# A two-layer streaming-encoder trunk on one Trainium2 core: a fixed schedule for the sums, roundings and low parts of the left operands in the up projection's background

## The chip, the cores and the metric

One NeuronCore of a Trainium2 chip runs the whole program in one launch. The metric is device time in microseconds (us), the median of the runs shown. The engines are named as in the profile: PE (TensorE, matmul), PEld (its weight load), DVE (VectorE), ACT (ScalarE), POOL (GpSimd) and SP (SyncE, which issues the DMAs).

## The reference, cut to what matters

The trunk has two layers over a sequence of 1024 rows of width 1024. Each layer adds an S5 group and a differential attention group, and then a convolutional gated feed-forward block. The change lies in the last one:

```python
def _conv_gated_ffn(h, w_up, w_conv, b_conv, w_down):
    seqlen = h.shape[1]
    up = h @ w_up
    padded = jnp.pad(up, ((0, 0), (CONV_WIDTH - 1, 0), (0, 0)))
    conv = b_conv + sum(w_conv[j] * padded[:, j:j + seqlen] for j in range(CONV_WIDTH))
    gate = conv[..., :FFN_DIM]
    val = conv[..., FFN_DIM:]
    return (jax.nn.silu(gate) * val) @ w_down
...
    for i in range(DEPTH):
...
        h = _rmsnorm(x, norm_ffn[i])
        x = x + _conv_gated_ffn(h, w_up[i], w_conv[i], b_conv[i], w_down[i])
    return _rmsnorm(x, norm_final)
```

## The kernel before, in words

Every fp32 operand of a large matmul is split into a rounded high part (ACT, a copy to fp32r) and a low part (DVE or POOL, the operand less its high part). Three matmuls then make one product of two splits: high by high, high by low, low by high (`mm3`, L440 to L442).

**The up projection** (`up`, L1366) works on 22 tiles f of 128 channels of the gate and the same 128 of the value. Each tile is a two by two block product done with seven block products instead of eight, in the order of `UP_ORDER`: 11, 12, s2, s1, s3, 22, s4. A block product is 4 times `mm3`, 12 matmuls of 128x512. The results are collected in `u0` and `u1` in SBUF: ACT copies the accumulator `upa` out after 11, s2 and s3; DVE adds or subtracts `upb` after 12, `upc` after s3 and s4, and `upd` after 22. The accumulator `upa` goes on after each copy, so product s2 may start only when ACT has copied product 11 out. Likewise `upc`, made by product s1 and read by DVE after s3, goes on in product s4, so s4 may start only when DVE has read it.

**The background.** After each of the seven products of a tile the program calls `bg.tick()`, which takes every queued generator one step further. `gate(f)` (L1402) is queued at the end of tile f and runs in the ticks of tile f+1: the convolution of the value half after product 11 (one ACT instruction with the centre tap, two DVE scalar_tensor_tensor), that of the gate half after product 12, Silu on ACT after s1, and the product of both on DVE after s3. When f is odd, a pair (f-1, f) of gated tiles is complete. It then becomes a left operand of the down projection, which also uses seven products, and `Seven.spill` (L331) prepares that operand: four sums of blocks (s1 = 21 + 22, s2 = s1 - 11, s3 = 11 - 21, s4 = 12 - s2), for each of the seven operands (11, 12, s2, s3, s1, 22, s4) a rounding on ACT and a low part on DVE, and a store to DRAM through SP. The spill of one pair starts in the tick of product 22 of the tile after the odd one and takes nine ticks. Below, the tile in which a spill starts is called the first tile, and the next one, in which it ends, the second. Nine pairs per layer are spilled; the last four tiles go another way.

**The right operands** are prepared at the same time for weights needed some seven products later, in the same split: ACT rounds, POOL makes the four sums and the seven low parts of each tile (`Ring`, `Seven.value` and `split`, L226).

**What sets the order.** The program text gives each tick's steps; a scheduler then puts the instructions of each engine into one list, which the engine executes in order. That list is fixed when the program is built, so what stands in it is known before any run.

Of the kernel before, what the change touches and what calls it, by code (L numbers as in the profile page):

```python
# [10 lines left out]
F32R = mybir.dt.float32r  # L11
BF16 = mybir.dt.bfloat16
I32 = mybir.dt.int32
AF = mybir.ActivationFunctionType
# [30 lines left out]
TAIL = list(range(2 * NPAIR, NF))  # L45
UP_ORDER = ["11", "12", "s2", "s1", "s3", "22", "s4"]
DN_ORDER = ["11", "12", "s2", "s3", "s1", "22", "s4"]
PARTNER = {"11": "11", "12": "21", "s4": "22", "22": "t4", "s1": "t1", "s2": "t2", "s3": "t3"}


@with_exitstack
def trunk_kernel(ctx: ExitStack, tc: tile.TileContext, A: dict, out: bass.AP, dbg: dict):
# [12 lines left out]
    def s4(name):  # L65
        return P4.tile([128, 1024], F32, tag="s4", name=name)
# [29 lines left out]
    def act(o, i, f, **kw):  # L96
        return nc.scalar.activation(o, i, f, **kw)  # L97

    def tt(o, a, b, op):
        V.tensor_tensor(o, a, b, op=op)  # L100
# [7 lines left out]
    MUL, ADD, SUB = ALU.mult, ALU.add, ALU.subtract  # L108
# [7 lines left out]
    class Tasks:  # L116
# [3 lines left out]
        def store(self, dst, src):  # L120

            self.late.append((dst, src))
# [32 lines left out]
    store = bg.store  # L155
# [125 lines left out]
    class Seven:  # L281
# [48 lines left out]

        def spill(self, dst):  # L331

            todo, summed, rounded = list(DN_ORDER), None, None
            while todo or summed or rounded:
                if rounded:
                    (n, v, d), rounded = rounded, None
                    self.eng(n).tensor_tensor(d[:, 512:1024].bitcast(F32R), v, d[:, 0:512], op=SUB)  # L337
                    store(dst[n], d)
                if summed:
                    (n, v), summed = summed, None  # L340
                    d = s4("ao")
                    act(d[:, 0:512].bitcast(F32R), v, AF.Copy)
                    rounded = n, v, d
                if todo:
                    n = todo.pop(0)
                    summed = n, self.value(n)
                yield

    class Held:
# [46 lines left out]
    for l in range(DEPTH):  # L396
# [26 lines left out]
        for np_ in PAIRS:  # L423
            sv = []
            for p in range(p0, p0 + np_):
# [3 lines left out]
                sv.append(Seven(W, "t", src, h[1], lambda name: G))  # L429
            for n in DN_ORDER:  # L430
                for q in range(np_):
                    sv[q].job(sv[q].srcs["11" if n == "11" else "22"][0], PARTNER[n])
            p0 += np_
# [5 lines left out]
    def mm3(o, l, r, first, last, go_on=False):  # L439
        PE.matmul(o, l[0], r[0], start=first, stop=False, skip_group_check=go_on)  # L440
        PE.matmul(o, l[0], r[1], start=False, stop=False, skip_group_check=go_on)  # L441
        PE.matmul(o, l[1], r[0], start=False, stop=last, skip_group_check=go_on)  # L442
# [29 lines left out]
    def gbc(src, name):  # L472
        g = s4(name)
        dma(g, src.partition_broadcast(128))
        return g
# [36 lines left out]
    def rope_tables():  # L512
# [7 lines left out]
        for h in range(2):  # L520
# [12 lines left out]
    xd = [DR.tile([128, 1024], F32, name=f"xd{i}") for i in range(8)]  # L533
    ad = [[{n: DR.tile([128, 1024], F32, name=f"ad{l}_{p}_{n}") for n in DN_ORDER} for p in range(NPAIR)]
          for l in range(2)]
# [642 lines left out]
    for l in range(DEPTH):  # L1178
# [84 lines left out]
        gf = gbc(A["norm_ffn"][l], "gf")  # L1263
        B = {n: Pieces("b" + n, 2, 512) for n in PARTNER.values()}

# [85 lines left out]
        def product(o, n, first):  # L1351
            w = W.take()[0]
            for k in range(4):
                mm3(o, tuple(v[:, 128 * k:128 * k + 128] for v in w), B[PARTNER[n]].get(k, 0, 512),
                    first and k == 0, k == 3, not first)
# [75 lines left out]
        for np_ in PAIRS:  # L1431
            for n in DN_ORDER:
                for p in range(p0, p0 + np_):
# [28 lines left out]
        for np_ in PAIRS:  # L1462
            chain = None
            for n in DN_ORDER:
                As, Bs = A7.take(np_), W.take(np_)
# [5 lines left out]
                for t in range(4):  # L1471
                    if n in ("12", "22"):
                        o = (smt if t % 2 else bgt)("dn")
                    else:
                        o = chain[t // 2][:, 512 * (t % 2):512 * (t % 2) + 512]
# [6 lines left out]
                    lo, hi = slice(0, 512), slice(512, 1024)  # L1482
# [71 lines left out]
```

## Time and profile before

| | us |
|---|---|
| median of 3 runs | 2517.65 (2516.12 to 2517.66) |
| the profiled execution's own time | 2518.42 |
| its span, first to last instruction | 2516.7 |
| PE busy in the span | 2332.9 (93%) |
| DVE busy | 1762.1 (70%) |
| POOL busy | 1160.1 (46%) |
| ACT busy | 1112.7 (44%) |

The busy shares are averages over stages with different limits. A row of a timeline gives start, duration, engine, line, operation, output <- inputs, and in brackets the idle time of the engine just before and what ended it. Names have their buffer numbers left out: `w` on DVE is the pair of sums s1 and s2 of a spill, `ao` a split operand of a spill, `g` a gated tile, `c` a convolution's result, `op` a split weight.

### The profile page before, as it was taken

The page shows a single profiled execution, that of the slowest core. Times are in us where ns is not written, and L with a number is a line of the kernel's source. Part 1 is how long each engine was busy: PE and PEld are TensorE (multiplying, and loading weights), DVE is VectorE, ACT ScalarE, POOL GpSimd, SP SyncE. Part 2 cuts the span into 40 slices and gives each one's busy share as a digit, 9 for nine tenths or more (in the row PEclk, how much of TensorE's full clock was granted, in tenths as well). Part 3 has the DMA queues.
Part 4 walks back from the last instruction along what each step waited for, and adds up shares of the span by engine and source line. Part 5 has one row for each costly group of instructions (what it writes and reads, how often), then busy time and mean ns, then how long its engine had stood idle before and what let it go on. Part 6 is the DMA issues. An engine that isn't in the chain of part 4 may idle for free. (4 is left out here: it accounts for less than half of the span.)

```text
span 2516.7 us, 34975 instructions
## 1 busy us (share of the span) xinstructions
PE 2332.9 (93%) x12180; PEld 1933.9 (77%) x12180; DVE 1762.1 (70%) x3249; ACT 1112.7 (44%) x2164; POOL 1160.1 (46%) x853
## 2 busy tenths in 40 slices
PE   5899999997999999999988999999979999999998
PEld 4777987785887777777777788877858777777776
DVE  7987567658777878456579775675687787864645
ACT  4455266434555555322135642754245555552221
POOL 3210011035777878777022101012267788878750
PEclk8999999998999999999999999999989999999999
DMA  6344731421344435886134447214113444549651
GB/s 178 118 114 120 204 105 47 159 80 42 109 150 130 161 129 176 305 302 228 54 97 153 112 136 218 68 51 155 67 42 129 147 151 135 166 168 360 226 183 67
DMA packets 295753, 361.42 MB, mean 144 GB/s; under 512 B 43160, under 2 KB 230136, under 8 KB 295576
## 3 DMA queue, kind: packets, MB, share of 16 engines
q1 hardware_dynamic: 295576, 359.18, 43.5%
q8 instruction: 97, 1.59, 0.3%
q14 instruction: 80, 0.66, 0.1%
HBM read 235.36 MB, written 123.73 MB: 143 GB/s over the span
## 5 line engine op out<-in xcount | busy, mean ns | idle before, releaser
L231 POOL TENSOR_TENSOR op<-st,op 128x512 fp32r<-128x512 f32 x112 | 168.9, 1538 | 889.1 <-ACT op L97 815.2
L231 POOL TENSOR_TENSOR op<-wu,op 128x512 fp32r<-128x512 f32 x220 | 321.1, 1480 | 160.9 <-ACT op L97 159.0
L106 DVE SCALAR_TENSOR_TENSOR c<-u,cv,c 128x1023 f32<-128x1023 f32 (+1 forms) x176 | 230.2, 1310 | 57.0 <-ACT c L97 52.9
L440 PE MATMUL rw<-op,hTh 128*128 128x256 f32 x768 | 228.0, 297 | 8.3 <-ACT hTh L97 3.6
L441 PE MATMUL rw<-op,hTh 128*128 128x256 f32 x768 | 225.1, 293 | 1.6 <-POOL op L231 1.6
L442 PE MATMUL rw<-op,hTl 128*128 128x256 f32 x768 | 223.3, 291 | 0.0
L100 DVE TENSOR_TENSOR xf<-xf,dnc 128x512 f32<-128x512 f32 (+1 forms) x160 | 124.7, 792 | 132.0 <-PE dnc L442 121.9
L231 POOL TENSOR_TENSOR op<-w,op 128x512 fp32r<-128x512 f32 x124 | 175.0, 1422 | 24.9 <-ACT op L97 24.9
L97 ACT ACTIVATE c<-u,cv 128x1024 f32<-128x1024 f32 x88 | 106.7, 1212 | 149.6 <-DVE u L100 143.9
L231 POOL TENSOR_TENSOR op<-wd,op 128x512 fp32r<-128x512 f32 x106 | 138.1, 1322 | 68.2 <-ACT op L97 67.7
L440 PEld LDWEIGHTS rw<-op,hTh 128*128 128x128 f32 x768 | 151.4, 197 | 10.9 <-ACT hTh L97 4.0
L440 PE MATMUL dnc<-op,aop 128*128 128x512 f32 x360 | 146.6, 413 | 12.4 <-DVE xf L100 12.1
L441 PEld LDWEIGHTS rw<-op,hTh 128*128 128x128 f32 x768 | 151.4, 197 | 4.4 <-POOL op L231 2.5
L442 PEld LDWEIGHTS rw<-op,hTl 128*128 128x128 f32 x768 | 151.1, 197 | 0.7 <-issue 0.6
L441 PE MATMUL dnc<-op,aop 128*128 128x512 f32 x360 | 141.7, 394 | 0.0
L100 DVE TENSOR_TENSOR u<-u,upc 128x512 f32<-128x512 f32 x88 | 60.0, 681 | 115.3 <-ACT u L97 109.2
L442 PE MATMUL dnc<-op,aop 128*128 128x512 f32 x360 | 139.7, 392 | 0.0
L97 ACT ACTIVATE u<-upa 128x512 f32<-128x512 f32 x132 | 78.0, 591 | 139.1 <-PE upa L442 137.1
L97 ACT ACTIVATE op<-wu 128x512 fp32r<-128x512 f32 x220 | 129.0, 620 | 0.0
L337 DVE TENSOR_TENSOR ao<-g,ao 128x512 fp32r<-128x512 f32 x90 | 117.4, 1320 | 15.7 <-ACT ao L97 15.7
L97 ACT ACTIVATE op<-wd 128x512 fp32r<-128x512 f32 x106 | 62.3, 625 | 148.9 <-PE dnc L442 64.0
L97 ACT ACTIVATE e<-sc,anm 128x256 f32<-128x256 f32 (+7 forms) x128 | 94.1, 738 | 62.9 <-DVE anm L103 48.8
(341 smaller groups left out, 7133.1 us busy)
## 6 DMA issues: line engine op xcount, KB each, us to landing
wu<-in_w_up_dram SPq DMA_DIRECT2D x88, 512.0 KB
ad_s<-ao SPq DMA_DIRECT2D x72, 512.0 KB
aop<-ad_s SPq DMA_DIRECT2D x72, 512.0 KB
ad<-ao SPq DMA_DIRECT2D x54, 512.0 KB
aop<-ad SPq DMA_DIRECT2D x54, 512.0 KB
wd<-in_w_down_dram SPq DMA_DIRECT2D x44, 512.0 KB
st<-in_w_in_dram SPq DMA_DIRECT2D x32, 256.0 KB
st<-in_w_in_dram SPq DMA_DIRECT2D x16, 512.0 KB
```

The costliest lines, as they stand in the source:

```text
L97: return nc.scalar.activation(o, i, f, **kw)
L100: V.tensor_tensor(o, a, b, op=op)
L106: return V.scalar_tensor_tensor(o, a, s, b, op0, op1)
L231: eng.tensor_tensor(lo.bitcast(F32R), src, hi, op=SUB)
L337: self.eng(n).tensor_tensor(d[:, 512:1024].bitcast(F32R), v, d[:, 0:512], op=SUB)
L440: PE.matmul(o, l[0], r[0], start=first, stop=False, skip_group_check=go_on)
L441: PE.matmul(o, l[0], r[1], start=False, stop=False, skip_group_check=go_on)
L442: PE.matmul(o, l[1], r[0], start=False, stop=last, skip_group_check=go_on)
```

## The change

The spill no longer takes its operands one by one in a pipeline of three stages. A table, `SPILL`, says for each of the nine ticks which sums, roundings and low parts are done in it. The third and fourth ticks, in which the next tile's convolutions are started, have none. The same instructions are issued, all on the same engines: 4 sums and 7 low parts on DVE, 7 roundings on ACT, 7 stores.

```diff
+SPILL = [[("sum", "s1"), ("hi", "11")], [("sum", "s2"), ("lo", "11"), ("hi", "12")], [], [],
+         [("lo", "12"), ("sum", "s3"), ("hi", "s2")], [("lo", "s2"), ("sum", "s4"), ("hi", "s3")],
+         [("lo", "s3"), ("hi", "s1")], [("lo", "s1"), ("hi", "22"), ("hi", "s4")], [("lo", "22"), ("lo", "s4")]]
...
         def spill(self, dst):
 
-            todo, summed, rounded = list(DN_ORDER), None, None
-            while todo or summed or rounded:
-                if rounded:
-                    (n, v, d), rounded = rounded, None
-                    self.eng(n).tensor_tensor(d[:, 512:1024].bitcast(F32R), v, d[:, 0:512], op=SUB)
-                    store(dst[n], d)
-                if summed:
-                    (n, v), summed = summed, None
-                    d = s4("ao")
-                    act(d[:, 0:512].bitcast(F32R), v, AF.Copy)
-                    rounded = n, v, d
-                if todo:
-                    n = todo.pop(0)
-                    summed = n, self.value(n)
+            b, d = self.block, {}
+            self.tmp = s4("w7")
+            x, y = self.tmp[:, 0:512], self.tmp[:, 512:1024]
+            v = {"11": b("11"), "12": b("12"), "s1": x, "s2": y, "s3": b("21"), "22": b("22"), "s4": b("12")}
+            sums = {"s1": (x, b("21"), b("22"), ADD), "s2": (y, x, b("11"), SUB),
+                    "s3": (b("21"), b("11"), b("21"), SUB), "s4": (b("12"), b("12"), y, SUB)}
+            for step in SPILL:
+                for what, n in step:
+                    if what == "sum":
+                        o, p, q, op = sums[n]
+                        tt(o, p, q, op)
+                    elif what == "hi":
+                        d[n] = s4("ao")
+                        act(d[n][:, 0:512].bitcast(F32R), v[n], AF.Copy)
+                    else:
+                        tt(d[n][:, 512:1024].bitcast(F32R), v[n], d[n][:, 0:512], SUB)
+                        store(dst[n], d.pop(n))
                 yield
```

**DVE, from the first tile's products 22 and s4 into the second tile's product 12**, in the kernel before. The `u` rows with `upc`, `upd` and `upc` belong to products s3, 22 and s4 of the first tile, the one with `upb` to product 12 of the second; `c_8426` and `c_8456` are the two convolutions of the first tile.

```order
L100 TENSOR_TENSOR u_8262<-u_8262,upc 128x512
L337 TENSOR_TENSOR ao<-g,ao 128x512
L100 TENSOR_TENSOR u_8262<-u_8262,upd 128x512
L106 SCALAR_TENSOR_TENSOR c_8426<-u_8262,cv,c_8426 128x1023
L100 TENSOR_TENSOR u_8261<-u_8261,upc 128x512
L106 SCALAR_TENSOR_TENSOR c_8426<-u_8262,cv,c_8426 128x1022
L106 SCALAR_TENSOR_TENSOR c_8456<-u_8261,cv,c_8456 128x1023
L308 TENSOR_TENSOR w_8423<-g 128x512
L337 TENSOR_TENSOR ao<-g,ao 128x512
L309 TENSOR_TENSOR w_8423<-w_8423,g 128x512
L100 TENSOR_TENSOR u_8402<-u_8402,upb 128x512
```

The same place in the changed kernel (`u_8261` is now what `u_8262` was, and so on):

```order
L103 TENSOR_TENSOR w_8382<-g 128x512
L103 TENSOR_TENSOR u_8261<-u_8261,upc 128x512
L103 TENSOR_TENSOR w_8382<-w_8382,g 128x512
L103 TENSOR_TENSOR ao<-g,ao 128x512
L103 TENSOR_TENSOR u_8261<-u_8261,upd 128x512
L103 TENSOR_TENSOR ao<-g,ao 128x512
L103 TENSOR_TENSOR g<-g 128x512
L103 TENSOR_TENSOR g<-g,w_8382 128x512
L109 SCALAR_TENSOR_TENSOR c_8427<-u_8261,cv,c_8427 128x1023
L103 TENSOR_TENSOR u_8260<-u_8260,upc 128x512
L109 SCALAR_TENSOR_TENSOR c_8427<-u_8261,cv,c_8427 128x1022
```

All four sums and the low parts of 11 and 12 now stand ahead of the convolution's first scalar_tensor_tensor, the sums s3 and s4 and the low part of 12 though the table gives them to the fifth and sixth ticks; in the kernel before one low part stood there.

**DVE, in the second tile**, between the adding of `upb` (product 12) and of `upc` (product s3), in the kernel before:

```order
L100 TENSOR_TENSOR u_8402<-u_8402,upb 128x512
L319 TENSOR_TENSOR g<-g 128x512
L106 SCALAR_TENSOR_TENSOR c_8456<-u_8261,cv,c_8456 128x1022
L337 TENSOR_TENSOR ao<-w_8423,ao 128x512
L337 TENSOR_TENSOR ao<-g,ao 128x512
L337 TENSOR_TENSOR ao<-w_8423,ao 128x512
L325 TENSOR_TENSOR g<-g,w_8423 128x512
L100 TENSOR_TENSOR g<-g,c_8426 128x1024
L100 TENSOR_TENSOR u_8403<-u_8403,upc 128x512
```

and in the changed kernel:

```order
L103 TENSOR_TENSOR u_8408<-u_8408,upb 128x512
L103 TENSOR_TENSOR ao<-w_8382,ao 128x512
L103 TENSOR_TENSOR ao<-g,ao 128x512
L103 TENSOR_TENSOR g<-g,c_8427 128x1024
L103 TENSOR_TENSOR u_8409<-u_8409,upc 128x512
L103 TENSOR_TENSOR ao<-w_8382,ao 128x512
L103 TENSOR_TENSOR ao<-g,ao 128x512
L103 TENSOR_TENSOR u_8409<-u_8409,upd 128x512
L103 TENSOR_TENSOR ao<-g,ao 128x512
```

Two sums, one low part and a convolution step have left the stretch ahead of the adding of `upc`.

**ACT, the convolutions of the first tile and the copy of product 11 of the second**, in the kernel before:

```order
L97 ACTIVATE op_8404<-wu 128x512
L97 ACTIVATE c_8426<-u_8262,cv 128x1024
L97 ACTIVATE c_8456<-u_8261,cv 128x1024
L97 ACTIVATE u_8402<-upa 128x512
L97 ACTIVATE ao<-g 128x512
L97 ACTIVATE op_8433<-wu 128x512
```

and in the changed kernel:

```order
L100 ACTIVATE op_8410<-wu 128x512
L100 ACTIVATE c_8427<-u_8261,cv 128x1024
L100 ACTIVATE c_8452<-u_8260,cv 128x1024
L100 ACTIVATE u_8408<-upa 128x512
L100 ACTIVATE op_8434<-wu 128x512
L100 ACTIVATE op_8456<-wu 128x512
```

The copy of product 11 stands right behind the second convolution in both; a rounding of the spill has left the place behind it.

## Rows read from the trace of the kernel before

**Rows 1.** The profile page, busy us (share of the span) by engine.

```profile
PE 2332.9 (93%) x12180; PEld 1933.9 (77%) x12180; DVE 1762.1 (70%) x3249; ACT 1112.7 (44%) x2164; POOL 1160.1 (46%) x853
```

**Rows 2.** Windows, one pair of tiles; behind the engines granted clock, DMA share, GB/s.

```profile
756.50:796.30 39.80, 38.69 (x169) 31.39 (x169) 30.92 (x30) 21.35 (x34) 31.87 (x23) 1.00 0.44 146
```

**Rows 3.** PE's waits over the whole span: us in total, times, longest us.

```profile
PE upc L440 <- DVE u L100: 18.8, 20, 1.1
...
PE upa L440 <- ACT u L97: 3.3, 18, 0.2
```

**Rows 4.** PE's timeline: start us, duration us, and in brackets the idle time before.

```profile
804.91 0.50 PE L440 MATMUL upa<-bt2h,op 128*128 128x512 f32 x1 [0.19 <-ACT u L97]
...
818.67 0.39 PE L440 MATMUL upa<-b11h,op 128*128 128x512 f32 x1
...
824.11 0.39 PE L440 MATMUL upa<-bt2h,op 128*128 128x512 f32 x1
...
834.76 0.39 PE L442 MATMUL upd<-bt4h,op 128*128 128x512 f32 x1
836.07 0.50 PE L440 MATMUL upc<-b22h,op 128*128 128x512 f32 x1 [0.92 <-DVE u L100]
836.40 0.39 PE L441 MATMUL upc<-b22l,op 128*128 128x512 f32 x1
...
844.14 0.39 PE L442 MATMUL upb<-b21h,op 128*128 128x512 f32 x1
844.71 0.50 PE L440 MATMUL upa<-bt2h,op 128*128 128x512 f32 x1 [0.18 <-ACT u L97]
```

**Rows 5.** DVE's timeline in the same pair.

```profile
814.06 0.69 DVE L100 TENSOR_TENSOR u<-u,upc 128x512 f32<-128x512 f32 x1 [4.69 <-ACT u L97]
...
818.34 1.29 DVE L106 SCALAR_TENSOR_TENSOR c<-u,cv,c 128x1023 f32<-128x1023 f32 x1 [1.28 <-ACT c L97]
819.54 0.68 DVE L100 TENSOR_TENSOR u<-u,upc 128x512 f32<-128x512 f32 x1
...
823.29 0.68 DVE L337 TENSOR_TENSOR ao<-g,ao 128x512 fp32r<-128x512 f32 x1
823.90 1.78 DVE L309 TENSOR_TENSOR w<-w,g 128x512 f32<-128x512 f32 x1
825.60 0.68 DVE L100 TENSOR_TENSOR u<-u,upb 128x512 f32<-128x512 f32 x1
...
834.21 1.21 DVE L100 TENSOR_TENSOR g<-g,c 128x1024 f32<-128x1024 f32 x1
835.34 0.68 DVE L100 TENSOR_TENSOR u<-u,upc 128x512 f32<-128x512 f32 x1
```

**Rows 6.** POOL's timeline in the same pair.

```profile
814.62 4.26 POOL L231 TENSOR_TENSOR op<-wu,op 128x512 fp32r<-128x512 f32 x3 [2.86 <-ACT op L97]
818.84 1.28 POOL L308 TENSOR_TENSOR w<-wu 128x512 f32<-128x512 f32 x1
820.21 1.29 POOL L309 TENSOR_TENSOR w<-w,wu 128x512 f32<-128x512 f32 x1
823.30 1.83 POOL L231 TENSOR_TENSOR op<-wu,op 128x512 fp32r<-128x512 f32 x1 [1.80 <-ACT op L97]
```

**Rows 7.** ACT's timeline, the gate half's convolution and the copy of product 11.

```profile
803.13 1.21 ACT L97 ACTIVATE c<-u,cv 128x1024 f32<-128x1024 f32 x1 [1.95 <-DVE u L100]
804.28 0.58 ACT L97 ACTIVATE u<-upa 128x512 f32<-128x512 f32 x1
```

**Rows 8.** PE's timeline behind two idle stretches in other stages.

```profile
113.33 0.41 PE L737 MATMUL w<-ident,ws 128*128 128x128 f32 x2 [3.33 <-DVE ws L100]
...
1196.64 0.50 PE L440 MATMUL dnc<-op,aop 128*128 128x512 f32 x1 [1.93 <-DVE xf L100]
```

**Rows 9.** Windows behind each of these two, columns as in rows 2.

```profile
113.34:114.28 0.94, 0.94 (x6) 0.47 (x6) 0.94 (x2) 0.36 (x1) 0.94 (x1) 1.00 0.22 55
...
1197.20:1200.61 3.41, 3.41 (x9) 2.65 (x8) 0.52 (x1) 0.60 (x2) 0.00 (x0) 0.50 0.00 0
```

## The prediction

> **What bounds the kernel now.** The page comes first: PE is busy 93% of the span, more than any other engine [rows 1]. The stage that the change touches is the up projection, so I cut one pair of its tiles out with the windows. In 39.80 us PE is busy 38.69, at a granted clock of 1.00, which is 2.4 GHz [rows 2]. The stage is thus bound by the stream of matmuls, and DVE, ACT and POOL count only where PE waits for them. Then PE's waits: 20 times for DVE's work on `u` ahead of a matmul into `upc`, 18.8 us in all, and 18 times for ACT's copy ahead of one into `upa`, 3.3 us [rows 3]. Last the timelines, to see where these sit. Undisturbed, 24 matmuls take 824.11 - 818.67 = 5.44 us, 0.227 each, 2.72 a block product [rows 4].
>
> Both waits stand in each pair with a spill, nine per layer; a tenth of the first kind, at the end of a layer's tiles, has no spill of the change's kind around it and I leave it. (1) In the second tile product s4 starts 836.07 - 834.76 = 1.31 us after the matmul ahead of it instead of 0.23, and its second matmul follows after 0.33 instead of 0.23 [rows 4]: 1.18 us lost. DVE reads `upc` only at 835.34, right behind the gated product that began at 834.21 [rows 5], because its list holds the spill's work before that. (2) In the following first tile, product s2 starts 0.57 instead of 0.23 us after its forerunner, and the same slow restart follows [rows 4]: 0.45 us. Together 1.63 us per pair.
>
> **The change, part by part.** Nothing is added or removed: 4 sums, 7 low parts, 7 roundings and 7 stores per spill stay on the same engines. What moves is their place in DVE's list.
>
> *Taken out of the second tile.* Two sums, one low part and one convolution step leave the stretch ahead of the reading of `upc`, and more has left earlier. DVE's list there now holds, from the first convolution step, three more such steps, two `u` additions, two low parts and the gated product. By the durations below that is about 10.7 us from the convolution's start, with the wait for ACT in it, and PE needs it some 12.5 us after that start. So wait (1) goes, 1.18 us per pair, with about 2 us to spare. Wait (2) goes as well: `upd` is read behind two low parts, and the convolutions and the copy behind them still end about 1 us ahead of product s2.
>
> *Put into the first tile.* Five spill instructions now stand between DVE's reading of `upc` after s3 and the first convolution step: the sum s2, the low parts of 11 and 12, the sums s3 and s4 (s1's sum falls into DVE's idle 4.69 us ahead [rows 5]). Before, one stood there. What such an instruction takes depends on POOL. With POOL waiting for ACT up to 823.30 [rows 6], a low part starting at 823.29 takes 0.68, and the next instruction starts 0.61 later. With POOL at work, the sum at 823.90 takes 1.78, and the next starts 1.70 later [rows 5]. Instructions that read PSUM keep 0.68 in both cases [rows 5]. I call the 1.70 held. The Trainium skill, "SBUF — State Buffer", section "SBUF: two separate sides", has a rule for this, and it speaks against the change: a DVE instruction with two SBUF inputs and a POOL instruction that reads SBUF share a port that one holds for its whole instruction while the other is blocked. By that rule read strictly each of the five would wait for a full POOL instruction, 1.29 us by the row of an undisturbed one [rows 6], where the rows show 1.70 - 0.61 = 1.09; the sum would rise by 5 x 1.29 - 4.5 x 1.09 = 1.5 us per pair, 28 us in all. The sum goes by the rows.
>
> Will POOL be at work there? From 814.62 it does three low parts, and two sums from 818.84 to about 821.5 [rows 6]. In the changed list a third sum follows before the first low part that needs a new rounding, so six instructions stand ready. Held, each takes about 1.70 as well, 10 us in all, so POOL covers the stretch. Between the low parts of 11 and 12 DVE does the subtraction of `upd`, 0.60 without the port, and POOL gets that much ahead: there I put 1.10 for 1.70.
>
> From A = 814.06, where DVE reads `upc` after s3 [rows 5]: that addition 0.60, sum s2 1.70, low part 11 1.70, `upd` 0.60, low part 12 1.10, sums s3 and s4 3.40. The convolution's first step starts at A + 9.10; before, it started at 818.34 = A + 4.28 [rows 5]. Behind it are 1.20 for the step (819.54 - 818.34), 0.68 for the addition after s4 with 0.03 to ACT, 1.15 from ACT's start on the gate half's convolution to the copy of product 11 (804.28 - 803.13 [rows 7]), and 0.63 from the copy's start to PE's product s2 (804.91 - 804.28 [rows 4, 7]). Product s2 starts at A + 12.79. PE is ready for it at 824.11 = A + 10.05 [rows 4]. It idles 2.74 us, with the restart's 0.10 2.84 per pair, where it lost 1.63. For 18 pairs that is 18 x 1.21 = **21.8 us** lost.
>
> *The ends of that.* If all five are held in full: 0.60 more per pair, 33 us. If none is held: 5.0 us less than above, no new wait, and the old ones gone: 18 x 1.63 = 29 us won.
>
> *The clock.* So far PE's idle 0.92 in this stage left the clock at 1.00 [rows 2, 4]. An idle stretch of 2.74 - 0.16 = 2.58, counted as there, is new to it. After 1.93 us idle at 1196.64 the granted clock was 0.50, 1.2 GHz, for 3.41 us; after 3.33 at 113.33 it stayed 1.00 [rows 8, 9]. At half the clock 3.41 us hold half the work: 1.7 us lost each time. None to all 18 is 0 to 31 us. The rows go both ways, so I take one in three: 6 x 1.7 = **10.2 us**.
>
> *At nothing.* Roundings move with the low parts; ACT is busy 21.35 of 39.80 us [rows 2]. The two sums' tile is taken one or two products earlier, a store and some weight loads change places on SP's queue; PE waits for no weight in this stage, whose operands are made some seven products ahead, about 19 us.
>
> **Sum.** 2518.42 (the profiled execution's time) + 21.8 + 10.2 = 2550.4; the median of the runs shown lies 0.8 below that execution, so **2550 us**. A measurement can tell some 0.2%, 5 us, from no change.
>
> **The rivals.**
> - *The clock falls after every new wait*: 2550 + 12 x 1.7 = 2570. For it: the idle is longer than the 1.93 that was followed by a fall. Against: 3.33 was not.
> - *The port is not contended there*, and the change wins. POOL idles while DVE does the five. Both old waits go, 2517.65 - 29 = 2488. It decides at 3.4 held instructions of five: then the new wait, 2.74 - 1.1 x 1.09, costs as much as the old ones. For it: POOL waits for ACT's roundings 2.86 and 1.80 us twice in a pair [rows 6]. Against: the stretch lies after the first and ahead of the second.
> - *They cancel*, 2513 to 2523: three to four held, the clock kept.
> - *Full blocking.* Each of the five waits for a whole undisturbed POOL instruction, 1.29 us [rows 6], instead of 1.09 for four and a half of them: 2550 + 28 = 2578. This is the skill's rule of above read strictly. For it: DVE's held instruction never shared, it waited. Against: the 1.70 of the rows.
> - *A second wait.* Product s4 of the second tile is late as well, 18 x 1.18 = 21 more, 2571. For it: DVE has 30.92 busy us of 39.80 [rows 2]. Against: two sums and a low part have left there.
> - *The change doesn't do what it says.* In part this is in the list: the sums s3 and s4 and the low part of 12, due in ticks five and six, stand ahead of the convolution. It is the reason for the forecast, not a further case.
>
> **Chances.** The forecast, a new wait of 2.2 to 3.4 us with the clock falling now and then, 2530 to 2563: 0.70. Clock falling each time: 0.10. Full blocking: 0.05. A second wait: 0.04. Cancelling: 0.05. Winning: 0.06. The range of 8 in 10 goes from 2526, about four held and no fall, to 2574. Faster by over 0.2%: 0.06; within 0.2%: 0.05; slower: 0.89.
>
> **What would show it.** PE's waits for DVE ahead of `upc` would fall from 20 to about 2, and those for ACT ahead of `upa` stay at 18 but rise from 0.2 to about 2.6 us each. DVE's sums s2, s3 and s4 would each take about 1.78, and stand ahead of the convolution. The windows of some pairs would show a clock below 1.00. I am wrong if these sums take 0.68 (no holding), if the first convolution step starts within 6 us of the reading of `upc`, or if wait (1) is still there.

## The result and the profile after

The changed kernel took **2546.37 us** (median of 4 runs, 2543.03 to 2546.89), against 2517.03 (2516.12 to 2517.66) for the kernel before, measured with it. The ratio is 1.011, 95% interval 1.0094 to 1.0125: slower by 29.3 us. The forecast was 2550, slower. The profiled execution of the changed kernel took 2546.44 us, 28.0 more than the profiled one before.

The page's busy times show no more work, only a longer span [rows 1]:

```profile
PE 2335.1 (92%) x12180; PEld 1941.6 (76%) x12180; DVE 1782.3 (70%) x3249; ACT 1106.5 (43%) x2164; POOL 1160.8 (46%) x853
```

PE is busy 2.2 us more than before, and DVE 20.2 us more with the same instructions: some of them last longer.

Where the 28.0 us lie is seen in the windows. I cut out the up projection of each layer, from its 61st matmul, past a start at half the clock, to its last (columns as in [rows 2]: length, busy us of PE, PEld, DVE, ACT and POOL, granted clock, DMA share, GB/s):

```profile
613.86:1052.37 438.51, 411.38 (x1788) 335.49 (x1787) 327.42 (x301) 224.73 (x352) 337.44 (x237) 1.00 0.42 139
1866.21:2304.73 438.52, 411.46 (x1789) 335.48 (x1787) 327.36 (x301) 224.74 (x352) 337.48 (x237) 1.00 0.42 139
```

The same two stretches before were 426.26 and 426.13 us long. So 24.6 of the 28.0 us are lost here, and PE's busy time in them did not rise (411.4 us against 412.5 before): the loss is idle time. PE's waits in the changed kernel name it (columns as in [rows 3]):

```profile
PE upa L446 <- ACT u L100: 46.7, 18, 2.6
PE upc L446 <- DVE u L103: 2.2, 2, 1.1
```

Of the waits ahead of `upc` two are left, where there were 20. Those ahead of `upa` are still 18, but 2.6 us each instead of 0.2. One of them in PE's timeline, with the matmul ahead of it:

```profile
791.46 0.39 PE L448 MATMUL upb<-b21h,op 128*128 128x512 f32 x1
794.45 0.50 PE L446 MATMUL upa<-bt2h,op 128*128 128x512 f32 x1 [2.60 <-ACT u L100]
794.79 0.39 PE L447 MATMUL upa<-bt2l,op 128*128 128x512 f32 x1
```

The operand `bt2` is that of product s2. The stretch that this wait ends shows on DVE as follows, from the reading of `upc` after product s3 of the first tile:

```profile
781.70 0.69 DVE L103 TENSOR_TENSOR u<-u,upc 128x512 f32<-128x512 f32 x1 [5.04 <-ACT u L100]
782.30 1.75 DVE L103 TENSOR_TENSOR w<-w,g 128x512 f32<-128x512 f32 x1
783.97 1.77 DVE L103 TENSOR_TENSOR ao<-g,ao 128x512 fp32r<-128x512 f32 x1
785.67 0.68 DVE L103 TENSOR_TENSOR u<-u,upd 128x512 f32<-128x512 f32 x1
786.27 1.18 DVE L103 TENSOR_TENSOR ao<-g,ao 128x512 fp32r<-128x512 f32 x1
787.38 1.77 DVE L103 TENSOR_TENSOR g<-g 128x512 f32<-128x512 f32 x1
789.07 1.77 DVE L103 TENSOR_TENSOR g<-g,w 128x512 f32<-128x512 f32 x1
790.77 1.27 DVE L109 SCALAR_TENSOR_TENSOR c<-u,cv,c 128x1023 f32<-128x1023 f32 x1
791.96 0.67 DVE L103 TENSOR_TENSOR u<-u,upc 128x512 f32<-128x512 f32 x1
```

In order: sum s2, low part of 11, the subtraction of `upd`, low part of 12, sums s3 and s4, and only then the convolution's first step. POOL works through nearly the whole stretch, and ACT's copy of product 11 comes right behind the convolution that waited for DVE:

```profile
782.21 4.70 POOL L234 TENSOR_TENSOR op<-wu,op 128x512 fp32r<-128x512 f32 x3 [3.15 <-ACT op L100]
786.86 1.74 POOL L311 TENSOR_TENSOR w<-wu 128x512 f32<-128x512 f32 x1
788.68 1.62 POOL L312 TENSOR_TENSOR w<-w,wu 128x512 f32<-128x512 f32 x1
790.26 1.73 POOL L322 TENSOR_TENSOR wu<-wu 128x512 f32<-128x512 f32 x1
```

```profile
792.67 1.21 ACT L100 ACTIVATE c<-u,cv 128x1024 f32<-128x1024 f32 x1 [5.07 <-DVE u L103]
793.82 0.58 ACT L100 ACTIVATE u<-upa 128x512 f32<-128x512 f32 x1
```

That it is so pair after pair, the groups by line and tile show (DVE, 712 to 1052 us, columns count, busy us, mean ns, idle us before): seven sums s3 and seven sums s4, all long, and no idle time ahead of them.

```profile
L103 DVE TENSOR_TENSOR g<-g,w 128x512 f32<-128x512 f32 x7 | 12.4, 1774 | 0.0
L103 DVE TENSOR_TENSOR g<-g 128x512 f32<-128x512 f32 x7 | 12.4, 1774 | 0.0
```

Last the windows of one whole pair, and of the 3.41 us behind three of the 18 waits: the first and the second of layer 1, and the first of layer 2.

```profile
712.50:753.48 40.98, 38.38 (x168) 31.45 (x169) 32.01 (x30) 21.02 (x34) 31.90 (x22) 1.00 0.44 141
669.97:673.38 3.41, 3.41 (x8) 2.73 (x9) 3.38 (x4) 3.41 (x7) 2.79 (x3) 0.50 0.02 5
712.50:715.90 3.40, 3.40 (x15) 2.82 (x16) 3.37 (x4) 3.40 (x7) 2.77 (x3) 1.00 0.00 0
1922.66:1926.07 3.41, 3.41 (x10) 2.67 (x9) 3.38 (x5) 3.41 (x7) 3.18 (x3) 0.50 0.00 0
```

A pair takes 40.98 us instead of 39.80 [rows 2], and the granted clock fell behind the first new wait of each layer and behind no other: 2 of 18.

### The profile page after: what moved, and what is told of

Same layout as the page of the kernel before. It is cut to its first block, busy times and chain, and to the rows that moved or that the text cites. A ratio compares the mean times of both kernels' runs of the same rounds, so it can differ in the third digit from the quotient of the medians.

```text
span 2544.5 us, 35015 instructions
## 1 busy us (share of the span) xinstructions
PE 2335.1 (92%) x12180; PEld 1941.6 (76%) x12180; DVE 1782.3 (70%) x3249; ACT 1106.5 (43%) x2164; POOL 1160.8 (46%) x853
## 5 line engine op out<-in xcount | busy, mean ns | idle before, releaser
L234 POOL TENSOR_TENSOR op<-wu,op 128x512 fp32r<-128x512 f32 x220 | 310.9, 1434 | 184.6 <-ACT op L100 184.6
L234 POOL TENSOR_TENSOR op<-w,op 128x512 fp32r<-128x512 f32 x124 | 166.8, 1358 | 24.7 <-ACT op L100 24.6
L103 DVE TENSOR_TENSOR ao<-g,ao 128x512 fp32r<-128x512 f32 x90 | 132.2, 1469 | 4.9 <-ACT ao L100 4.9
```

What stands on the lines that cost most here:

```text
L234: eng.tensor_tensor(lo.bitcast(F32R), src, hi, op=SUB)
```

## The experiments

The theory is the prediction's: DVE's sums and low parts ahead of the first tile's convolution, each lengthened by POOL at work, delay the convolution, with it ACT's copy of product 11, and so product s2 of the next tile. The rivals are that the order costs something else (ACT's list, stores, weights), or that a sum moved away only moves the wait. Nine runs were made, two of them (e7, e9) of the changed kernel again. Each time stands beside runs of the kernel before on the same chip; its median there was 2519.28 us (e1 to e4), 2519.51 (e5 to e7) and 2518.64 (e8, e9).

For each, the up projection's length in layers 1 and 2, cut out of its trace as above, and the new wait of a pair:

| | us, median | stage, layer 1 | layer 2 | wait, us each, and product |
|---|---|---|---|---|
| before | 2517.03 | 426.26 | 426.13 | 0.9 s4, 0.2 s2 |
| the change | 2546.37 | 438.51 | 438.52 | 2.6 s2 |
| e1 | 2508.46 | 421.67 | 421.69 | 0.9 s2 |
| e2 | 2499.65 | 417.03 | 416.68 | 0.4 s3 |
| e3 | 2521.84 | 427.42 | 427.36 | 1.5 s3 |
| e4 | 2480.78 | 407.81 | 407.81 | none |
| e5 | 2477.38 | 407.84 | 407.81 | none |
| e6 | 2488.35 | 410.87 | 410.83 | none |
| e8 | 2600.42 | 463.57 | 464.51 | 3.6 s2 |

### e1: the sum s4 behind the convolution

`steps` collects the convolutions' last instructions; `issue_after` puts an instruction behind one of them in the scheduler's list. The work is the same.

```diff
-            stt(c[:, 2:], u[:, :1022], cv[:, 0, ft:ft + 1], c[:, 2:], MUL, ADD)
+            steps.append(stt(c[:, 2:], u[:, :1022], cv[:, 0, ft:ft + 1], c[:, 2:], MUL, ADD))
...
                 for what, n in step:
-                    if what == "sum":
+                    late = (what, n) == ("sum", "s4")
+                    if late and what != "hi":
+                        with tc.issue_after(steps[-1].ins):
+                            if what == "sum":
+                                o, p, q, op = sums[n]
+                                tt(o, p, q, op)
+                            else:
+                                tt(d[n][:, 512:1024].bitcast(F32R), v[n], d[n][:, 0:512], SUB)
+                        if what == "lo":
+                            store(dst[n], d.pop(n))
+                    elif what == "sum":
```

> The changed kernel, with the sum s4 alone queued on DVE behind the first tile's last convolution step. Theory (DVE's list puts five spill instructions ahead of the convolution, each held by POOL for 1.70 us): one held instruction fewer, so the new wait of 2.6 us per pair shrinks by 1.7 to about 0.9, the old waits do not come back, and the clock has no idle stretch left to fall after. Loss per pair 1.04 + 0.10 instead of 1.63 in the kernel before: 18 x -0.5 = -9 us, about 2508. Rival (ACT is late, because two roundings of the spill stand ahead of the convolution on ACT): nothing changes, about 2546. Rival (the loss is the clock falling after idle stretches): only the falls go, about 2540.

Measured: 2508.46 us (2508.17 to 2509.13), 0.9959 of before (0.9944 to 0.9975). PE's wait in its trace:

```profile
PE upa L456 <- ACT u L100: 16.2, 18, 0.9
```

The idle ahead of product s2 fell from 2.60 to 0.90 us, by 1.70: the time from one held sum's start to the next instruction (789.07 to 790.77 in the changed kernel). The stage is shorter by 33.7 us over the two layers, about 18 x 1.70 = 30.6 and the two falls of the clock behind the new waits (1.7 each), which are gone too. One sum put back beyond the convolution makes the change a gain.

### e2: the sums s3 and s4 behind the convolution

The same edit with one line changed:

```diff
-                    late = (what, n) == ("sum", "s4")
+                    late = (what, n) in (("sum", "s3"), ("sum", "s4"))
```

> The changed kernel, with the sums s3 and s4 queued on DVE behind the first tile's last convolution step. Theory: two held instructions fewer, 3.4 us, more than the wait has; the wait ahead of product s2 goes entirely. In the second tile the rounding of s3 then comes late on ACT, ahead of Silu and the copy of product s2, so product s3 may wait some 0.6 us. Loss per pair 0 to 0.7 instead of 1.63: 2488 to 2501. Rival (ACT's roundings ahead of the convolution): about 2546.

Measured: 2499.65 us (2496.46 to 2500.81), 0.992 of before (0.990 to 0.9939).

```profile
PE upa L456 <- ACT u L100: 6.8, 18, 0.6
```

The second sum does not bring another 1.7 us per pair, since only 0.90 of the wait were left. What remains, 0.4 us in 17 of the 18 pairs and 0.6 in one, stands ahead of product s3 (operand `bt3`) and no longer ahead of s2, a new and smaller wait in place of the old one:

```profile
747.29 0.50 PE L456 MATMUL upa<-bt3h,op 128*128 128x512 f32 x1 [0.36 <-ACT u L100]
```

### e3: the table as it is written

All sums and low parts of the fifth and later ticks are put behind the convolution, where the table has them:

```diff
-                    late = (what, n) == ("sum", "s4")
+                    late = SPILL.index(step) >= 4
```

> The changed kernel with every sum and low part of the table's fifth to ninth ticks queued on DVE behind the first tile's last convolution step, as the table has it. Theory: the wait ahead of product s2 goes, but the same held instructions now stand in the second tile, and a wait of 1 to 2 us per pair appears there, ahead of product s3 or s4: loss per pair about 1.6 to 1.9 against 1.63, so 2515 to 2525. Rival (the table's placement itself is what helps, and only the scheduler's hoisting spoils it): all waits go, about 2488.

Measured: 2521.84 us (2517.31 to 2525.03), 1.0009 of before (1.0000 to 1.0019). The wait ahead of s2 is gone, and one ahead of product s3 (`bt3`) has come:

```profile
795.61 0.50 PE L456 MATMUL upa<-bt3h,op 128*128 128x512 f32 x1 [1.54 <-ACT u L100]
```

ACT's list just ahead of it tells why:

```profile
793.52 0.63 ACT L100 ACTIVATE ao<-g 128x512 fp32r<-128x512 f32 x1 [3.41 <-DVE g L103]
794.06 1.00 ACT L100 ACTIVATE g<-c 128x1024 f32<-128x1024 f32 x1
794.97 0.59 ACT L100 ACTIVATE u<-upa 128x512 f32<-128x512 f32 x1
```

The rounding of s3 (`ao<-g`) stands ahead of Silu and of the copy of `upa` and waits 3.41 us for its sum, which DVE now makes after the convolution. So the order the table describes would not have been a gain either: late sums hold up ACT, early ones hold up DVE. This also sets e1 and e2 in their place: they gain because they move little.

### e4 and e5: POOL out of the way

In the changed kernel (e4) and in the kernel before (e5), the low parts of the up projection's weights are left out. POOL fills the tile with a constant in their place, so the output lacks those low parts; PE's matmuls are the same in number.

```diff
+    def rounded(dst, src, eng):
+
+        hi, lo = dst[:, 0:512], dst[:, 512:1024]
+        act(hi.bitcast(F32R), src, AF.Copy)
+        eng.memset(lo, 0.0)
+        return hi.bitcast(F32R), lo.bitcast(F32R)
...
-            self.ring.job(need, lambda d: split(d, self.v.pop(name), self.eng(name)), pre)
+            self.ring.job(need, lambda d: (split if self.kind == "t" else rounded)(d, self.v.pop(name), self.eng(name)), pre)
```

> The changed kernel with DVE's list untouched. The low parts of the up projection's right operands are left out: POOL fills them with zeros, an instruction that reads no SBUF, instead of subtracting. Theory (holding by POOL): the spill's sums and low parts take 0.68 us except where they meet one of POOL's four remaining sums per tile, the convolution starts about 5 us after the reading of upc instead of 9.1, the wait ahead of product s2 goes, and so do the old ones: about 2488. Rival (the order alone, whatever an instruction takes, or ACT): the wait stays at 2.6 us and the time at about 2546. If both contribute, the wait shrinks in part.

> The kernel before the change, with the low parts of the up projection's weights left out and a constant fill of the same tile by POOL in their place (the output loses those low parts). This is the control to the same edit in the changed kernel (which took 2480.8 us). Theory (what the change costs is only that VectorE's sums ahead of the convolution are lengthened by POOL's subtractions): where POOL no longer holds up VectorE, it must not matter where the sums stand, so the old waits of up to 1.2 us also go and the time is 2470 to 2485 us, within 8 us of the changed kernel's with the same edit. Rival (the new order costs something apart from POOL, for instance by the issue order on ScalarE or later stores): the kernel before with this edit stays below the changed one by 15 us or more, under 2466 us. Second rival (the edit gains by something else than those waits, for instance a lighter POOL queue): the old waits ahead of the second tile's products s4 and s2 stay and the time stays above 2500 us.

Measured: e4 2480.78 us (2477.78 to 2484.27), 0.985 of before (0.9831 to 0.9868); e5 2477.38 us (2474.59 to 2484.74), 0.9843 (0.982 to 0.9865). In both no wait of a pair is left, and the stage takes 407.8 us in each layer of each. In e4, three of DVE's rows:

```profile
805.66 0.68 DVE L103 TENSOR_TENSOR w<-w,g 128x512 f32<-128x512 f32 x1
808.58 1.80 DVE L103 TENSOR_TENSOR g<-g 128x512 f32<-128x512 f32 x1
810.30 0.68 DVE L103 TENSOR_TENSOR g<-g,w 128x512 f32<-128x512 f32 x1
```

Sums s2 and s4, 1.75 and 1.77 us in the changed kernel, take 0.68. The convolution's first step starts 810.91 - 805.06 = 5.85 us after the reading of `upc`, where about 5 were expected and the changed kernel has 9.07. Only s3 still takes 1.80; it falls together with one of POOL's sums of weights, which are still there. POOL's rows at that place, with a fill (0.53 us) after the sum:

```profile
808.53 1.29 POOL L319 TENSOR_TENSOR w<-w,wu 128x512 f32<-128x512 f32 x1
809.89 0.53 POOL L241 MEMSET op<- 128x512 f32 x1
```

The control e5 shows no cost of the new order apart from POOL: with POOL light, old order and new give the same stage to 0.03 us, and the medians differ by 3.4 us, with ranges that overlap. It also shows that the old waits (1) and (2) had the same cause as the new one, since they go too. So the 12 us per layer between before and after are a matter of where the lengthened instructions stand. The fills also make POOL's list shorter, but that weights now come earlier is not the gain: PE waited for none in this stage before. Nor do the zeros make the matmuls quicker: a pair takes 38.08 us in e4 as in e6 below, whose weights are whole. Both times lie below the 2488 us at which the two old waits alone would be saved; small waits for `bt1` and its like in the first tiles, ahead of the pairs, went as well.

### e6: another table

The sums s3 and s4 behind the convolution as in e2, and the parts of s1 one product ahead of those of s3:

```diff
-         [("lo", "12"), ("sum", "s3"), ("hi", "s2")], [("lo", "s2"), ("sum", "s4"), ("hi", "s3")],
-         [("lo", "s3"), ("hi", "s1")], [("lo", "s1"), ("hi", "22"), ("hi", "s4")], [("lo", "22"), ("lo", "s4")]]
+         [("lo", "12"), ("sum", "s3"), ("hi", "s2")], [("lo", "s2"), ("sum", "s4"), ("hi", "s1")],
+         [("lo", "s1"), ("hi", "s3")], [("lo", "s3"), ("hi", "22"), ("hi", "s4")], [("lo", "22"), ("lo", "s4")]]
```

> The changed kernel with sums s3 and s4 put behind the first tile's last convolution step, and the rounding and low part of s1 put one product ahead of those of s3 (a version meant to beat both kernels). Theory (a pair loses what VectorE's late sums ahead of the second tile's first products add, each lengthened to about 1.77 us by POOL): with only s2 ahead of the convolution and s1's parts stored before s3's are due, the wait ahead of product s2 is at most 0.4 us and no other product of the second tile waits; some 18 x (2.6 - 0.4) = 40 us below the changed kernel, 2495 to 2507 us, about the time of the version with the two sums alone behind the convolution (2499.7 us). Rival (the sums behind the convolution push the low part of s3 past its product): a wait of over 1 us per pair ahead of a later product, 2515 us or more.

Measured: 2488.35 us (2485.19 to 2489.78), 0.9875 of before (0.9859 to 0.9891), below the expected 2495 to 2507. It computes the whole result and beats both kernels. Windows of one pair:

```profile
789.06:827.14 38.08, 38.08 (x170) 31.53 (x169) 32.35 (x30) 21.11 (x34) 32.17 (x22) 1.00 0.47 152
```

PE is busy all of it. This row gives what a pair takes without a wait, 38.08 us, and so what the waits cost: 39.80 - 38.08 = 1.72 per pair before, 40.98 - 38.08 = 2.90 in the changed kernel. The expectation counted 2.2 us won per pair; with 2.90 and without the falls of the clock it is 18 x 2.90 + 3.4 = 55.6, which from 2546.4 gives 2490.8. DVE is busy 32.35 us of the pair, more than in the changed kernel: its sums are as long as ever. They only stand where nothing waits for them.

### e7 and e9: the changed kernel again

Two more profiles of the changed kernel, for the clock.

> The changed kernel again, unchanged, for one more profile of it. It is to show whether the clock falls at the same new waits each time. Theory (which of the equal waits of 2.59 us brings the clock down hangs on how they happen to fall in time, not on the product or layer): 18 new waits of 2.6 us again, of which another number and other ones, 0 to 6, are followed by a stretch of 3.41 us at 0.50. Rival (it is a fixed place in the program, such as the first full pair of a layer): again exactly two, in the same pairs of layers 1 and 2.

> The changed kernel unchanged, for a third profile. If each of the new waits had its own chance of one in three or of 3 in 36, falls would come behind any of the 18; if the first of a layer alone is open and the others follow it at a fixed distance of 40.97 us, falls come behind the first new wait of a layer or behind none.

Measured: 2543.1 and 2544.38 us, and in both the 18 waits of 2.6 us again. The 3.41 us behind the first and the second wait of layer 1 and the first of layer 2, in e7:

```profile
670.08:673.50 3.42, 3.42 (x9) 2.68 (x10) 3.38 (x4) 3.42 (x7) 2.91 (x3) 0.50 0.02 5
712.57:715.98 3.41, 3.41 (x15) 2.84 (x16) 3.38 (x4) 3.41 (x7) 2.79 (x3) 1.00 0.00 0
1920.09:1923.50 3.41, 3.41 (x15) 2.83 (x16) 3.38 (x4) 3.41 (x7) 2.79 (x3) 1.00 0.00 0
```

In e9 the clock fell behind both first ones. Over the three profiles a fall came behind 5 of the 6 first waits of a layer and behind none of the 48 others. The rival that it is a fixed place falls with e7's layer 2, and a chance of its own for each wait does not fit 5 of 6 against 0 of 48. Waits that follow at the same distance of 40.97 us share one fate. Behind a first wait with a fall the second came 42.5 to 42.6 us later, in layer 2 of e7, where none came, 40.97 us later like all the others.

### e8: the copy twice

```diff
             product(a, "11", True)
             act(u0[:, lo], a, AF.Copy)
+            act(u0[:, lo], a, AF.Copy)
```

> The changed kernel with ScalarE's copy of product 11 (u<-upa, 0.58 us, the last step ahead of product s2) issued twice over in every tile. The second copy writes the same values. Two things are to be told apart. Path: the new wait of 2.59 us ends at this copy, which follows the convolution's start; if that chain is what the tensor engine waits for, the wait grows by one issue step of ScalarE, 0.50 us (793.82 to 794.30 in the changed kernel's trace), to about 3.1 us, and the time by 18 x 0.5 = 9 us to about 2555 us; if the wait were released by something else, or had slack, the time stays at 2546 us. Clock: in the two profiles of the changed kernel the clock fell behind the first new wait of a layer in three of four cases and behind none of the other 32, which stand 40.97 us apart. If a fall hangs on how long the wait is, the longer wait makes it fall behind most of the 18, another 1.7 us each, over 2570 us in all; if it hangs on when in time a wait comes, the changed distance of about 41.5 us between waits lets other waits than a layer's first be followed by a fall, 2 to 6 of 18, 2553 to 2565 us; if something singles out the first pair of a layer, again at most two, both first ones.

Measured: 2600.42 us (2594.97 to 2603.53), 1.0319 of before (1.0297 to 1.0341). PE's wait, and ACT's rows of one pair:

```profile
PE upa L446 <- ACT u L100: 64.8, 18, 3.6
```

```profile
801.43 1.21 ACT L100 ACTIVATE c<-u,cv 128x1024 f32<-128x1024 f32 x1 [5.08 <-DVE u L103]
802.58 0.58 ACT L100 ACTIVATE u<-upa 128x512 f32<-128x512 f32 x1
803.05 0.62 ACT L100 ACTIVATE op<-wu 128x512 fp32r<-128x512 f32 x1
803.57 0.58 ACT L100 ACTIVATE u<-upa 128x512 f32<-128x512 f32 x1
```

The wait grew by 1.00 us, not by 0.50: the scheduler put a rounding between the two copies, and all of it went into the wait. So the path by this copy has no slack. 18 x 1.00 makes 18 us, and the time rose by 54, of which 51 lie in the two stages. The other 33 in the stages are for the clock to explain. It fell behind 16 of the 18 waits, in 11 of them for 6.83 us. A pair with no fall, one with a fall of 3.41 us and one with a fall of 6.83 us, then the stretch at half the clock that begins in the last one's wait:

```profile
893.09:935.06 41.97, 38.38 (x168) 31.45 (x169) 32.04 (x30) 21.98 (x36) 31.90 (x23) 1.00 0.43 138
935.06:978.65 43.59, 39.99 (x168) 32.58 (x168) 32.02 (x30) 22.08 (x36) 31.87 (x23) 0.96 0.41 133
715.07:759.69 44.62, 41.02 (x169) 33.38 (x169) 32.03 (x30) 22.09 (x36) 31.86 (x23) 0.92 0.40 130
713.93:720.76 6.83, 5.69 (x13) 4.46 (x14) 6.54 (x6) 4.76 (x10) 6.07 (x5) 0.50 0.27 111
```

By these rows a long fall costs 44.62 - 41.97 = 2.65 us and a short one 43.59 - 41.97 = 1.62: 11 x 2.65 + 5 x 1.62 = 37, less the 3 of the two falls that the changed kernel has, 34. The stages leave 51 - 18 = 33. Some 3 of the 54 us lie outside the stages and are not accounted for. Of the three readings on record for the clock, that a fall hangs on how long the wait is has its numbers (most of the 18, over 2570 us); the other two, at most 6 falls, are out for waits of 3.6 us. The edit also changed the distance between the waits, from 40.97 us to between 42.0 and 44.8, so that length alone is the cause is not shown.

## Why the prediction was right

Sign, size and mechanism came out as forecast, 2546.4 for 2550. By its steps:

- **Wait (1) goes, with slack.** Of 20 waits ahead of `upc` 2 are left, the number forecast. The slack is smaller than the 2 us forecast, 1.2: DVE has read `upc` at 803.57 + 0.69 = 804.26 and PE starts product s4 at 805.46. These are 13.5 and 14.7 us after the convolution's start, where 10.7 and some 12.5 were counted.

```profile
803.57 0.69 DVE L103 TENSOR_TENSOR u<-u,upc 128x512 f32<-128x512 f32 x1 [2.65 <-ACT u L100]
805.46 0.39 PE L446 MATMUL upc<-b22h,op 128*128 128x512 f32 x1
```

- **The first tile's stretch.** The convolution's first step was forecast at A + 9.10 and starts at 790.77 - 781.70 = A + 9.07. Product s2 was forecast at A + 12.79 and starts at A + 12.75; the idle time ahead of it was forecast as 2.58 and is 2.60. The low part of 12, to which 1.10 was given because POOL gets ahead of DVE during `upd`, took 787.38 - 786.27 = 1.11 to the next start.
- **Held by POOL.** Here the Trainium skill, "SBUF — State Buffer", section "SBUF: two separate sides", had spoken of a full block for a whole POOL instruction. That POOL holds DVE up, e4 and e5 bear out: without POOL's subtractions all four sums take 0.68 us in e5, and in e4 all but the one that meets a sum of POOL's. The size is that of the rows, 1.70 from start to start, 1.09 more than unheld; the strict reading with 1.29, rival "full blocking" at 2578, is out. POOL is at work over the whole stretch as forecast: its six instructions there last from 782.21 to 791.99, 9.8 us for the 10 counted.
- **The wait term.** Forecast 18 x 1.21 = 21.8 us; measured 18 x (40.98 - 39.80) = 21.2.
- **The clock term was over-sized.** Forecast were 6 falls of 1.7 us, 10.2 us. There were 2, 3.4 us, in the profiled run, and 1 and 2 in two more. This is the step that failed in size: "one in three" was a guess from two rows, and took the waits as independent draws. One of the two rows was misread besides. Behind the 3.33 us of idle time the clock stayed at 1.00 for the 0.94 us of work that the window shows [rows 9], but in the kernel before it fell 0.90 us later:

```profile
115.18:118.59 3.41, 0.00 (x0) 0.00 (x0) 3.41 (x7) 2.11 (x4) 3.41 (x1) 0.50 0.57 172
```

PE was idle again by then, so the trace doesn't tell which idle stretch brought the clock down, and the row is no evidence for a clock that stays. For a clock that stays after an idle stretch as long as the new one the prediction thus had no row, and that only 2 of the 18 waits brought it down was luck. The terms as measured, 21.2 + 3.4, are the 24.6 of the two stages.

- **A term that was not in the sum.** The other 3.4 of the 28.0 us lie outside the two stages, 2.25 of them ahead of the first (613.86 instead of 611.61). The up projection's very first matmul starts at 577.98 instead of 575.33. In the nine further profiles that one starts anywhere from 574.66 (e2) to 579.53 (e3), for the changed kernel again at 577.90 and 576.38, so this is about what profiles differ by there, and no cause is claimed. By luck it hid half of the clock term's excess: 2550.4 - 6.8 - 0.6 + 3.4 = 2546.4.
- **The rivals.** *The clock falls after every new wait* is out for 2.6 us and nearly what e8 shows for 3.6. *The port is not contended*, *they cancel* and *a second wait* are out by the timelines. (For *none held* the prediction takes off 5.0 us; its own terms give 4 x 1.09 + 0.49 = 4.85.) That *the change doesn't do what it says* was called the reason for the forecast: e1 and e2 show that the two sums ahead of their place make the loss, but e3 that the table, as written, would have gained nothing either.

## What to carry to other kernels

An instruction that another engine can lengthen is to be counted at its lengthened time, and its place matters more than its number: the same sums and low parts of a pair cost 2.90 us with all sums ahead of a convolution on PE's path, 1.72 in the old order, spread over two places, and nothing where nobody waits (e6). To find the path, count from the last event that both orders share, step by step, to the matmul that waits. After building a schedule from a table, read the list it made: a step's place in the table does not bind the scheduler, and a later place has its own price on the engine that waits next (e3).

## What the runs showed of the hardware

The clock did not fall in proportion to idle time or to the number of waits. The new waits of 0.9 us in e1 and of 1.5 us in e3 were followed by no fall. Waits of 2.6 us were followed by one 5 times in 54, all behind the first wait of a layer. Waits of 3.6 us were followed by one 16 times in 18, 11 of them twice as long as any behind 2.6 us. One more us per wait thus cost nearly 3 us of time.

Neither length nor place in the program decides it alone. Near the start of each stage PE waits 0.9 us for `bt1`, in nine of the eleven traces (not in e4 and e5). In 4 of these 18 places a fall of 3.41 us followed: in layer 1 of e1 and e8, and in layer 2 of e3 and e7. Here is the stretch behind the same wait of layer 2, first in e7 (wait ended at 1867.88) and then in the changed kernel's first profile (ended at 1870.03):

```profile
1868.16:1871.57 3.41, 3.41 (x9) 2.66 (x9) 3.41 (x4) 0.40 (x2) 3.41 (x3) 0.50 0.00 0
1870.31:1873.72 3.41, 2.76 (x11) 1.71 (x10) 3.41 (x4) 0.91 (x2) 3.41 (x3) 1.00 0.08 23
```

Such a fall cost next to nothing. In e1 the stage takes 421.67 us with it in layer 1 and 421.69 without it in layer 2, where two waits of 0.4 and 0.5 us for `bt4` follow that are missing in layer 1. Why the clock falls behind the first wait of a layer and not behind those that follow it at a fixed distance, these runs leave open.
